# In-projection of a hybrid encoder block: the recurrence's transfers and last products issued by GpSimd, the value norms made beside the memory's keys, two fixed value tiles, the second values last

## The chip, the core and the metric

The kernel runs on 1 core of one Trainium2 chip. Its five engines run side by side, each an instruction stream of its own in a fixed order: TensorE (PE: matrix products; PEld is its weight loading), VectorE (DVE), ScalarE (ACT), GpSimd (POOL) and SyncE (SP). SyncE only issues transfers (DMAs) here; GpSimd computes and issues some. An engine whose next instruction waits, for an operand, a buffer or a transfer, holds everything behind it. The metric is the device time of one execution in microseconds (us). One execution was recorded by the hardware profiler; its rows are quoted below.

## The reference

One layer over 2048 tokens of width 1024, in float32, cut to what the change touches:

```python
xn = rmsnorm(h, norm_mix_g[l])
proj = xn @ w_in[l]
q, k, v, u, y = jnp.split(proj, [512, 1024, 1536, 2048], axis=-1)
q = rope(q, positions)
k = rope(k, positions)
attn = dilated_mixture_attention(q, k, v)
uc = centred_depthwise_conv(u, conv_w[l], conv_b[l])
rec = bidirectional_rglru(uc, ...) * gelu(y)
h = h + concatenate([attn, rec]) @ w_out[l]
```

`bidirectional_rglru` makes two gates of the convolved u in each direction, scans forward and backward over the 2048 tokens and adds the two scans. Cross-attention into 256 memory tokens, an MLP and a last norm follow; neither they nor the attention itself are touched.

## The kernel before

**Products.** Each float32 operand is split in a high part h (rounded by ACT) and a low part l (the rest, by VectorE or GpSimd), and each product is three: h h, l h, h l (`mm3`, L119 to L121). For the weights, SyncE loads 256 KB of w_in into a ring of three buffers `wraw` (L224), ACT makes wh (L225), and wl is made by GpSimd or VectorE in turn (L226).

**Stages of the first 704 us.** The tokens are taken in two blocks of 1024. Block 0's units U and Y come first (a unit is 256 columns of w_in, for 1024 tokens). Then `memory_kv` makes keys and values of the memory, whose last product ends at 141.3 us, and block 1's units U follow. Then come block 1's units Y, v0, k0, q0, v1, k1, q1, with the recurrence `lru` as side work: a generator from which each step of a unit draws 1.3 steps on average. Then x of block 0 is loaded and split again (`x_block`: L315, ACT L320, DVE L321), block 0's units v0 to k1 with the rest of `lru` follow, then the loads of attention head 0 (`load_head`: q and k by GpSimd, L175 and L178), and block 0's last unit q1. Attention's first scores are L750, on `kc`, copies of the keys by GpSimd (L696); L754 on VectorE takes them up.

**Order.** A scheduler sets each engine's order at build time, by the order in which the program is written and priorities; the banks of PSUM (m, b, a) and the buffers of each tile then decide who waits for whom.

**Value norms.** The v units need the sum of squares of each column of the scaled value weights. Before, unit v0 and unit v1 of block 1 each made them when their own weights came: ACT squares (L140, tile vsq), GpSimd adds (L142, vss), four one-column products with a ones vector (L149), a copy, rstd on GpSimd (L115, L116), and a row form through a diagonal dg (L160) and a product (L163, L164). A value tile v (L451) is divided into high and low halves in `vb` (one buffer: memset L454 by GpSimd, L456, L457) and stored by L460.

**Recurrence.** For each of 4 channel tiles (ct) and 4 chunks of 512 tokens, `conv` loads u (L485), makes uc (first tap GpSimd L489, three more VectorE L491) and splits it; `gates` makes products in bank a and ACT's tanh (tr L513, ti L516). Conv runs two chunks ahead of the gates. After each second chunk `forward` scans (L531), and at a channel tile's end `backward` scans back (L536), GpSimd adds the two (L539), gy is loaded (L543), VectorE multiplies (L544) and rec is stored (L545). All these transfers, and the gate weights gr (L469), are SyncE's; gy has two buffers, so a load waits until the rec stored from its buffer has landed.

**Rope.** q and k units are turned by VectorE (L376 to L381), split (rh by ACT L385, rl by VectorE L386) and stored by SyncE (L387, L388).

Of the kernel before, what the change touches and what calls it, by code (L numbers as in the profile page):

```python
# [11 lines left out]
AF = mybir.ActivationFunctionType  # L12
# [12 lines left out]
VW = 130  # L25
# [14 lines left out]
def hybrid_block(ctx: ExitStack, tc: tile.TileContext, prm, x, xT, mem, memT, pos, masks, w_in, gate_w,  # L40
# [61 lines left out]
    nhalf = small("nhalf", [P, 4])  # L102
    pool.memset(nhalf, -0.5)
    ones = small("ones", [P, 1])
    pool.memset(ones, 1.0)
    all1 = small("all1", [P, P])
    pool.memset(all1, 1.0)
    dsc = small("dsc", [P, 4])
    hpi = small("hpi", [P, 1])
# [96 lines left out]
    with ExitStack() as s12:  # L206
# [10 lines left out]
        def unit_steps(src, r, sums=None):  # L217
            for kk in range(2):
                h = wr.tile([P, 4, 256], F32R, tag="wh", name="wh", bufs=4)
                l = wr.tile([P, 4, 256], F32R, tag="wl", name="wl", bufs=4)  # L220
                r.append((h, l))
                for k in range(0, 4, 2):
                    t = wr.tile([P, 2, 256], F32, tag="wraw", name="wraw", bufs=3)
                    dma(t, src[:, 4 * kk + k:4 * kk + k + 2, :])  # L224
                    act.activation(h[:, k:k + 2, :], t, AF.Copy)  # L225
                    (dve if k else pool).tensor_tensor(l[:, k:k + 2, :], t, f32(h[:, k:k + 2, :]), op=ALU.subtract)  # L226
                    for i in range(2 if sums else 0):
                        c = 4 * kk + k + i
                        sums.add(t[:, i, :], gmix[:, c:c + 1])
                    yield  # L230

        def unit_w(src, lazy=False, sums=None):

            r = []
            steps = unit_steps(src, r, sums)
            get = lambda k, c: (r[k // 4][0][:, k % 4, c], r[k // 4][1][:, k % 4, c])
            if lazy:
                return get, steps
            for _ in steps:
                pass  # L240
            return get

# [189 lines left out]
        def v_unit(W, X, B, n2, step, sums):  # L432

            for th in range(2):
                for m2 in range(2):
                    o = ps("mmb")
                    v = p2.tile([P, 512], F32, tag="r0", name="v")
                    for z in range(2):
# [6 lines left out]
                        if sums:  # L445
                            sc = slice(2 * n2, 2 * n2 + 2)
                            sums.columns(svc[:, sc])
                            sums.rows(svr[n2], "a")
                            dve.reciprocal(dsc[:, sc], svc[:, sc])
                            sums = None  # L450
                        dve.scalar_tensor_tensor(v[:, 256 * z:256 * z + 256], oz, rsb[:, r:r + 1], svr[n2],  # L451
                                                 op0=ALU.mult, op1=ALU.mult)
                    vb = p2.tile([P, 8, VW], F16, tag="vb", name="vb", bufs=1)
# [1112 lines left out]
```

## Time and profile before

| what | value |
|---|---|
| median of 3 runs | 2867.53 us (2866.56 to 2873.28) |
| the profiled execution | 2870.64 us |
| its span, first to last instruction | 2868.9 us |
| mean granted TensorE clock | 0.952 |
| TensorE busy, 0 to 100 us | 88.5 us |
| memory's last product ends | 141.3 us |
| the projection's last product ends | 662.6 us |
| first scores begin | 691.0 us |

In the prediction's rows, a wait is read "engine, line, <- what came last: us in total, times, longest". A row of a group has the line, engine, operation, tiles written <- read, shape and count, then busy us and mean ns, then the idle time just before it and what ended it. In the windows, each engine has its busy us and, in brackets, its instructions; PEclk is the clock granted to TensorE as a share of full speed, DMA the busy share of the 16 DMA engines. A row of the timeline starts with the start time and the duration, in us. SPq is SyncE's queue.

### The profile page before, as it was taken

To read this page: it belongs to the slowest core of one execution; us is meant where nothing else is said; L and a number is where in the kernel's file an instruction comes from. 1 tells how busy PE (TensorE), PEld (TensorE's weight loads), DVE (VectorE), ACT (ScalarE), POOL (GpSimd) and SP (SyncE) were. 2 spreads that over 40 slices of the span, in tenths; PEclk is the share of its full clock that TensorE was granted. 3 is DMA by queue.
4 is the path that set the end of the run, shared out by engine and by line. 5 is a ranking of instruction groups with operands and counts; after the bars stand their busy time and mean duration, and the time that the engine had idled before them with its cause. 6 is when DMAs were issued, how large, how long until landed. Compare 5 with 4: busy or idle time off the path is not lost. (4 is left out here: it accounts for less than half of the span.)

```text
span 2868.9 us, 40008 instructions
## 1 busy us (share of the span) xinstructions
PE 2585.6 (90%) x14104; PEld 2186.2 (76%) x14104; DVE 2027.9 (71%) x3376; ACT 1285.1 (45%) x2366; POOL 1256.8 (44%) x884
## 2 busy tenths in 40 slices
PE   8899785884889998999997999899998999999997
PEld 6778675774889998787875788778886777777876
DVE  7547676764778878546578544665548999999997
ACT  6438545452556666335433333433333333333342
POOL 2222121211544442451145555646656766666662
PEclk9999897987889999899998999999999999999999
DMA  6433344336677784653243333343335222212213
GB/s 214 144 125 98 116 113 141 101 106 186 180 184 210 201 206 124 202 170 102 97 159 121 108 113 107 113 144 109 109 114 205 71 84 81 81 67 89 77 49 118
DMA packets 258045, 368.43 MB, mean 128 GB/s; under 512 B 85683, under 2 KB 132019, under 8 KB 254773
## 3 DMA queue, kind: packets, MB, share of 16 engines
q1 hardware_dynamic: 253556, 338.62, 37.4%
q0 software_dynamic: 4288, 27.27, 3.8%
q8 instruction: 111, 1.82, 0.3%
q14 instruction: 90, 0.73, 0.1%
HBM read 251.19 MB, written 114.63 MB: 128 GB/s over the span
## 5 line engine op out<-in xcount | busy, mean ns | idle before, releaser
L1299 ACT ACTIVATE c<-raw 128x512 fp32r<-128x512 f32 x162 | 101.8, 632 | 274.0 <-PE m L120 137.4
L1149 ACT ACTIVATE wh<-wr 128x512 fp32r<-128x512 f32 x128 | 80.9, 632 | 288.9 <-PE m L120 145.9
L1150 POOL TENSOR_TENSOR wl<-wr,wh 128x512 fp32r<-128x512 f32 x96 | 144.7, 1508 | 146.3 <-ACT wh L1149 146.3
L757 ACT ACTIVATE sm<-sm,obp 128x256 f32<-128x256 f32 (+1 forms) x384 | 161.4, 467 | 46.2 <-DVE obp L754 40.0
L1150 DVE TENSOR_TENSOR wl<-ws,wh 128x512 fp32r<-128x512 f32 x96 | 82.2, 856 | 126.5 <-ACT wh L1149 117.6
L754 DVE CUSTOM_DVE_ANT_0 sm<-a,msk 128x256 f32<-128x256 f32 (+1 forms) x384 | 131.0, 371 | 31.3 <-PE a L751 27.5
L226 POOL TENSOR_TENSOR wl<-wraw,wh 128x512 fp32r<-128x512 f32 x48 | 70.3, 1467 | 166.5 <-ACT wh L225 157.6
L1171 DVE TENSOR_TENSOR c<-m,c 128x512 f32<-128x512 f32 x64 | 44.2, 690 | 139.9 <-PE m L121 137.9
L769 ACT ACTIVATE ph<-b 128x512 f16<-128x512 f32 (+1 forms) x192 | 100.4, 523 | 95.2 <-PE b L766 90.3
L119 PE MATMUL m<-xh,wh 128*128 128x512 f32 x328 | 131.3, 400 | 7.4 <-ACT xh L320 7.4
L770 DVE SCALAR_TENSOR_TENSOR pl<-b,ph 128x512 f16<-128x512 f32 (+1 forms) x192 | 114.6, 598 | 28.4 <-ACT ph L769 24.5
L120 PE MATMUL m<-xl,wh 128*128 128x512 f32 x328 | 130.1, 397 | 0.7 <-DVE xl L321 0.7
L121 PE MATMUL m<-xh,wl 128*128 128x512 f32 x328 | 130.5, 398 | 0.0
L1300 POOL TENSOR_TENSOR wh<-raw,c 128x512 fp32r<-128x512 f32 x58 | 94.7, 1648 | 76.6 <-ACT c L1299 71.6
L696 POOL TENSOR_SCALAR kc<-kh 128x1024 fp32r<-128x1024 f32 x32 | 68.5, 2141 | 127.7 <-PE a L750 115.6
L766 PE MATMUL b<-prt,sm 128*128 128x128 f32 x640 | 107.8, 283 | 17.3 <-DVE pl L770 9.3
L750 PE MATMUL a<-kc,qb 128*128 128x256 f32 x256 | 108.5, 425 | 5.9 <-DVE obp L754 5.9
L1172 DVE SCALAR_TENSOR_TENSOR c<-c 128x512 f32<-128x512 f32 x96 | 112.4, 1171 | 1.0
L1149 ACT ACTIVATE wh<-ws 128x512 fp32r<-128x512 f32 x96 | 60.3, 628 | 109.0 <-PE m L120 108.0
L121 PE MATMUL m<-t3h,wl 128*128 128x512 f32 x276 | 107.7, 390 | 1.1 <-POOL wl L1150 1.1
L1300 POOL TENSOR_TENSOR wl<-raw,c 128x512 fp32r<-128x512 f32 x58 | 93.3, 1625 | 19.8 <-ACT c L1299 19.8
L751 PE MATMUL a<-kc,qb 128*128 128x256 f32 x256 | 101.6, 397 | 0.0
(571 smaller groups left out, 9731.0 us busy)
## 6 DMA issues: line engine op xcount, KB each, us to landing
wr<-in_w_m SPq DMA_DIRECT2D x64, 512.0 KB
hid_d<-c SPq DMA_DIRECT2D x128, 256.0 KB
wraw<-in_w_in SPq DMA_DIRECT2D x80, 256.0 KB
raw<-in_w_m SPq DMA_DIRECT2D x33, 512.0 KB
rawt<-hid_d SPq DMA_DIRECT2D x26, 512.0 KB
t0h<-hid_d SPq DMA_DIRECT2D x26, 512.0 KB
o_d<-obp SPq DMA_DIRECT2D x16, 528.0 KB
obr<-o_d SPq DMA_DIRECT2D x16, 528.0 KB
```

The costliest lines, as they stand in the source:

```text
L119: pe.matmul(o, ah, bh, start=start, stop=False, **kw)
L120: pe.matmul(o, ah, bl, start=False, stop=False, **kw)
L121: pe.matmul(o, al, bh, start=False, stop=stop, **kw)
L750: pe.matmul(so, q0, kh[:, w0:w0 + 256], start=True, stop=False)
L754: dve.tensor_tensor_reduce(out=sm, in0=sps[:, 256 * z + o0:256 * z + o0 + kw], in1=msk[:, m:m + kw], op0=ALU.add, op1=ALU.min, scale=1.0, ...
L757: exps.append(act.activation(sm, sm, AF.Exp, scale=-1.0, bias=self.obp[:, oc, 65:66]))
L766: pe.transpose(pt[:, c0:c0 + 128], self.sm[:, z, 128 * g:128 * g + 128], idt)
L770: dve.scalar_tensor_tensor(self.pl[:, :w], pt[:, :w], 1024.0, self.ph[:, :w], op0=ALU.mult, op1=ALU.subtract)
L1149: act.activation(h, self.a[n], AF.Copy)
L1150: last[n % 2] = (pool if n % 2 else dve).tensor_tensor(l, self.a[n], f32(h), op=ALU.subtract).ins
L1172: dve.scalar_tensor_tensor(z, z if n < 6 else o, 0.0, z, op0=ALU.max, op1=ALU.mult)
L1300: self.eng[n].tensor_tensor(l[-1], tk, f32(h[-1]), op=ALU.subtract)
```

## The change

- **Transfers.** The recurrence's transfers (gr, u, gy, rec; 52 in all) are issued by GpSimd (`dma_r`) instead of SyncE (`dma`), and the 16 products of gy by GpSimd instead of VectorE.
- **Value norms.** A new function `value_norms` is called twice after `memory_kv`, before block 1's U. It loads the two value weights once more (8 loads of 256 KB in the same ring), squares them in place (16 on ACT), and sums by 32 products of one column, with the squares as TensorE's weights. The v units no longer make norms.
- **Splits.** From the recurrence's stage on (`alone`), all wl splits go to VectorE; 28 leave GpSimd.
- **Value tiles.** `vb` becomes two fixed tiles, their ones set once.
- **Order of the units.** v0, k0, q0, k1, q1, v1 in place of v0, k0, q0, v1, k1, q1, so v1 is the unit behind head 0's loads; `last["store"]`, after which head 0's far value loads may issue, is now a store of block 0's q1, which comes before v1.
- **Small.** `ones` becomes a column of `all1`, small constants share a tile, and the banks of attention are named in another order.

The diff, with one line of context:

```diff
@@ -99,14 +99,13 @@
     cb, gb, lm, ifq = (col(n) for n in ("conv_b", "gate_b", "lam", "invf"))
-    nhalf = small("nhalf", [P, 4])
+    misc = small("misc", [P, 8])
+    nhalf, hpi = misc[:, 0:4], misc[:, 4:5]
     pool.memset(nhalf, -0.5)
-    ones = small("ones", [P, 1])
-    pool.memset(ones, 1.0)
     all1 = small("all1", [P, P])
     pool.memset(all1, 1.0)
+    ones = all1[:, 0:1]
     dsc = small("dsc", [P, 4])
-    hpi = small("hpi", [P, 1])
     pool.memset(hpi, TWO_PI / 4)
@@ -214,31 +213,49 @@
 
-        def unit_steps(src, r, sums=None):
-            for kk in range(2):
-                h = wr.tile([P, 4, 256], F32R, tag="wh", name="wh", bufs=4)
-                l = wr.tile([P, 4, 256], F32R, tag="wl", name="wl", bufs=4)
-                r.append((h, l))
-                for k in range(0, 4, 2):
-                    t = wr.tile([P, 2, 256], F32, tag="wraw", name="wraw", bufs=3)
-                    dma(t, src[:, 4 * kk + k:4 * kk + k + 2, :])
-                    act.activation(h[:, k:k + 2, :], t, AF.Copy)
-                    (dve if k else pool).tensor_tensor(l[:, k:k + 2, :], t, f32(h[:, k:k + 2, :]), op=ALU.subtract)
-                    for i in range(2 if sums else 0):
-                        c = 4 * kk + k + i
-                        sums.add(t[:, i, :], gmix[:, c:c + 1])
-                    yield
-
-        def unit_w(src, lazy=False, sums=None):
+        def unit_w(src, lazy=False):
 
             r = []
-            steps = unit_steps(src, r, sums)
+
+            def steps():
+                for kk in range(2):
+                    h = wr.tile([P, 4, 256], F32R, tag="wh", name="wh", bufs=4)
+                    l = wr.tile([P, 4, 256], F32R, tag="wl", name="wl", bufs=4)
+                    r.append((h, l))
+                    for k in range(0, 4, 2):
+                        t = wr.tile([P, 2, 256], F32, tag="wraw", name="wraw", bufs=3)
+                        dma(t, src[:, 4 * kk + k:4 * kk + k + 2, :])
+                        act.activation(h[:, k:k + 2, :], t, AF.Copy)
+                        (dve if k or alone[0] else pool).tensor_tensor(l[:, k:k + 2, :], t, f32(h[:, k:k + 2, :]),
+                                                                       op=ALU.subtract)
+                        yield
+
             get = lambda k, c: (r[k // 4][0][:, k % 4, c], r[k // 4][1][:, k % 4, c])
             if lazy:
-                return get, steps
-            for _ in steps:
+                return get, steps()
+            for _ in steps():
                 pass
             return get
+
+        def value_norms(p1, n2):
+
+            sm = RowSum(p1, 1, 256)
+            o = [ps("a") for _ in range(2)]
+            for k in range(0, 8, 2):
+                t = wr.tile([P, 2, 256], F32, tag="wraw", name="wraw", bufs=3)
+                dma(t, w_in[4 + n2][:, k:k + 2, :])
+                for i in range(2):
+                    act.activation(t[:, i, :], t[:, i, :], AF.Square, scale=gmix[:, k + i:k + i + 1])
+                for j in range(2):
+                    for i in range(2):
+                        pe.matmul(o[j][:, 0:1], t[:, i, 128 * j:128 * j + 128], ones, start=k + i == 0, stop=k + i == 7)
+            sc = slice(2 * n2, 2 * n2 + 2)
+            sm.r = svc[:, sc]
+            for j in range(2):
+                dve.tensor_copy(svc[:, 2 * n2 + j:2 * n2 + j + 1], o[j][:, 0:1])
+            rstd_of(sm.r, sm.r, 2)
+            sm.rows(svr[n2], "a")
+            dve.reciprocal(dsc[:, sc], svc[:, sc])
 
@@ -429,7 +446,7 @@
 
-        def v_unit(W, X, B, n2, step, sums):
+        def v_unit(W, X, B, n2, step):
 
@@ -442,16 +459,9 @@
                             mm3(oz, X[0][th][k][:, tk], X[1][th][k][:, tk], wh, wl, k == 0, k == 7)
-                        if sums:
-                            sc = slice(2 * n2, 2 * n2 + 2)
-                            sums.columns(svc[:, sc])
-                            sums.rows(svr[n2], "a")
-                            dve.reciprocal(dsc[:, sc], svc[:, sc])
-                            sums = None
                         dve.scalar_tensor_tensor(v[:, 256 * z:256 * z + 256], oz, rsb[:, r:r + 1], svr[n2],
                                                  op0=ALU.mult, op1=ALU.mult)
-                    vb = p2.tile([P, 8, VW], F16, tag="vb", name="vb", bufs=1)
-                    pool.memset(vb[:, :, 64:66], 1.0)
+                    vb = vbs[m2]
                     v3 = v.rearrange("p (h d) -> p h d", h=8)
@@ -466,7 +476,7 @@
                 gr = lr.tile([P, 4, P], F32, tag="u", name="gr", bufs=2)
-                dma(gr, gate_w[:, 4 * ct:4 * ct + 4, :])
+                dma_r(gr, gate_w[:, 4 * ct:4 * ct + 4, :])
                 gh = lr.tile([P, 4, P], F32R, tag="gh", name="gh")
@@ -482,7 +492,7 @@
                 t0 = 512 * zc - 2
-                dma(u[:, lo:hi], u_d[ct, :, t0 + lo:t0 + hi])
+                dma_r(u[:, lo:hi], u_d[ct, :, t0 + lo:t0 + hi])
                 uc = lr.tile([P, 512], F32, tag="uc", name="uc", bufs=3)
@@ -540,9 +550,9 @@
                     gy = lr.tile([P, 512], F32, tag="gy", name="gy", bufs=2)
-                    dma(gy, gy_d[ct, :, 1024 * c + 512 * z:1024 * c + 512 * z + 512])
-                    dve.tensor_tensor(gy, hf[:, sl], gy, op=ALU.mult)
-                    dma(rec_d[ct, :, 1024 * c + 512 * z:1024 * c + 512 * z + 512], gy)
+                    dma_r(gy, gy_d[ct, :, 1024 * c + 512 * z:1024 * c + 512 * z + 512])
+                    pool.tensor_tensor(gy, hf[:, sl], gy, op=ALU.mult)
+                    dma_r(rec_d[ct, :, 1024 * c + 512 * z:1024 * c + 512 * z + 512], gy)
 
@@ -570,7 +580,7 @@
         U, Y = [(0, "u", 0), (1, "u", 1)], [(2, "y", 0), (3, "y", 1)]
-        QKV = [(4, "v", 0), (6, "k", 0), (8, "q", 0), (5, "v", 1), (7, "k", 1), (9, "q", 1)]
+        QKV = [(4, "v", 0), (6, "k", 0), (8, "q", 0), (7, "k", 1), (9, "q", 1), (5, "v", 1)]
 
@@ -583,27 +593,25 @@
                 mark[0] = tc.cur_priority
-                vs = None
-                if kind == "v" and B == 1:
-                    vs = RowSum(p2, 1, 256, rings={
-                        "ss": lambda: p2.tile([P, 512], F32, tag="rl", name="vss", bufs=2),
-                        "dg": lambda: p2.tile([P, 512], F32, tag="rl", name="vdg", bufs=2),
-                        "sq": lambda: p2.tile([P, 512], F32, tag="rh", name="vsq", bufs=2)})
-                W = first if n == 0 and first else unit_w(w_in[wi], sums=vs)
+                W = first if n == 0 and first else unit_w(w_in[wi])
                 step = pace
...
                 elif kind == "v":
-                    v_unit(W, X, B, n2, step, vs)
+                    v_unit(W, X, B, n2, step)
                 else:
...
 
+        vbs = [p2.tile([P, 8, VW], F16, name=f"vb{i}") for i in range(2)]
+        for vb in vbs:
+            pool.memset(vb[:, :, 64:66], 1.0)
         none = iter(())
...
         due = [0.0]
+        alone = [False]
         with sb("xr") as xr_pool:
@@ -614,10 +622,13 @@
                 softplus()
+                for n2 in range(2):
+                    value_norms(p1, n2)
                 t1 = tables(1)
...
             side = lru(lr)
+            alone[0] = True
             block(1, X, t1, Y + QKV, side)
@@ -636,7 +647,7 @@
         mk = s3.enter_context(sb("mk"))
-        psum_phase("psum2", m0=2, r=1, a=3, b=2)
+        psum_phase("psum2", b=2, m0=2, a=3, r=1)
         pw = s3.enter_context(sb("pw"))
```

SyncE's queue from memory's last weight load on, before (w_cv is the memory's weights, vm_d the memory's values stored, w_in at L224 the weights of U):

```order
59 L224 DMA wraw<-in_w_cv 128x512
60 L224 DMA wraw<-in_w_in 128x512 x2
61 L302 DMA vm_d<-eh 256x1x128
62 L302 DMA vm_d<-el 256x1x128
63 L224 DMA wraw<-in_w_in 128x512 x2
64 L302 DMA vm_d<-eh 256x1x128
65 L224 DMA wraw<-in_w_in 128x512
66 L302 DMA vm_d<-el 256x1x128
67 L224 DMA wraw<-in_w_in 128x512
68 L302 DMA vm_d<-eh 256x1x128
```

The same place after the change (L246 is the load in `value_norms`; the weight load is now L227):

```order
60 L246 DMA wraw<-in_w_in 128x512 x2
61 L319 DMA vm_d<-eh 256x1x128
62 L319 DMA vm_d<-el 256x1x128
63 L246 DMA wraw<-in_w_in 128x512
64 L319 DMA vm_d<-eh 256x1x128
65 L319 DMA vm_d<-el 256x1x128
66 L319 DMA vm_d<-eh 256x1x128
67 L319 DMA vm_d<-el 256x1x128
68 L246 DMA wraw<-in_w_in 128x512 x2
69 L319 DMA vm_d<-eh 256x1x128
70 L319 DMA vm_d<-el 256x1x128
71 L246 DMA wraw<-in_w_in 128x512 x3
```

Eight loads for the norms now stand ahead of U's weight loads, which follow the last row, in the same ring of three buffers.

GpSimd's queue before, at the end of the second channel tile (L539 adds the two scans, L489 is a conv's first tap):

```order
66 L539 TENSOR_TENSOR ti<-ti 128x1024 x2
67 L454 MEMSET vb 128x8x2
68 L481 MEMSET u 128x2
69 L226 TENSOR_TENSOR wl<-wraw,wh 128x512 x2
70 L454 MEMSET vb 128x8x2
71 L489 TENSOR_SCALAR uc<-u,prt 128x512 x2
72 L226 TENSOR_TENSOR wl<-wraw,wh 128x512 x2
73 L489 TENSOR_SCALAR uc<-u,prt 128x512
```

The same place after the change, from behind the first add on (L549 is the second add, L553 and L555 the transfers of gy and rec, L554 the product, L499 the conv's first tap, L495 its u load):

```order
79 L554 TENSOR_TENSOR gy<-ti,gy 128x512 x2
80 L555 DMA rec_d<-gy 128x512 x2
81 L549 TENSOR_TENSOR ti<-ti 128x1024
82 L491 MEMSET u 128x2
83 L495 DMA u<-u_d 128x513
84 L553 DMA gy<-gy_d 128x512 x2
85 L554 TENSOR_TENSOR gy<-ti,gy 128x512
86 L555 DMA rec_d<-gy 128x512
87 L554 TENSOR_TENSOR gy<-ti,gy 128x512
88 L555 DMA rec_d<-gy 128x512
89 L553 DMA gy<-gy_d 128x512 x2
90 L499 TENSOR_SCALAR uc<-u,prt 128x512
```

Between the adds and the next conv's first tap there now stand the products, the stores and the next loads of gy, which GpSimd takes one by one.

GpSimd's queue before, at the loads of head 0 (q to qb, k to kh and kl, then the key copies kc):

```order
91 L226 TENSOR_TENSOR wl<-wraw,wh 128x512 x2
92 L539 TENSOR_TENSOR ti<-ti 128x1024 x2
93 L175 DMA qb<-q_d_64 128x2048
94 L178 DMA kh<-k_d_66 64x2048 x2
95 L178 DMA kl<-k_d_66 64x2048 x2
96 L696 TENSOR_SCALAR kc<-kh 128x1024
97 L696 TENSOR_SCALAR kc<-kl 128x1024
```

The same place after the change:

```order
113 L549 TENSOR_TENSOR ti<-ti 128x1024
114 L553 DMA gy<-gy_d 128x512 x2
115 L554 TENSOR_TENSOR gy<-ti,gy 128x512
116 L555 DMA rec_d<-gy 128x512
117 L554 TENSOR_TENSOR gy<-ti,gy 128x512
118 L555 DMA rec_d<-gy 128x512
119 L174 DMA qb<-q_d_64 128x2048
120 L177 DMA kh<-k_d_66 64x2048 x2
121 L177 DMA kl<-k_d_66 64x2048 x2
122 L707 TENSOR_SCALAR kc<-kh 128x1024
```

Head 0's loads now stand behind the last chain of gy and rec.

## The prediction

> **What bounds the kernel now.** I read the busy times on the page first.
>
> ```profile
> span 2868.9 us, 40008 instructions
> PE 2585.6 (90%) x14104; PEld 2186.2 (76%) x14104; DVE 2027.9 (71%) x3376; ACT 1285.1 (45%) x2366; POOL 1256.8 (44%) x884
> ```
>
> TensorE is the bound, idle for a tenth of the span. The busy times by window say where.
>
> ```profile
> core 0: us, PE busy (x) PEld busy (x) DVE busy (x) ACT busy (x) POOL busy (x), PEclk, DMA share, GB/s
> 200.00:300.00 100.00, 97.59 (x518) 83.49 (x517) 64.90 (x80) 70.95 (x100) 25.66 (x29) 1.00 0.36 100
> 300.00:400.00 100.00, 74.98 (x390) 64.13 (x389) 67.50 (x88) 53.39 (x81) 20.17 (x25) 0.88 0.32 97
> 400.00:500.00 100.00, 67.23 (x329) 55.90 (x328) 65.83 (x95) 54.66 (x81) 10.04 (x9) 0.81 0.47 149
> 500.00:600.00 100.00, 76.47 (x355) 63.41 (x354) 72.17 (x98) 53.66 (x73) 16.36 (x14) 0.86 0.35 103
> 660.00:710.00 50.00, 11.92 (x61) 10.41 (x60) 17.27 (x42) 10.76 (x19) 4.60 (x6) 0.62 0.63 180
> ```
>
> While the recurrence runs beside the projection (300 to 600 us) TensorE is busy 67 to 76%, and the granted clock falls to 0.81; from 660 to 710 it hardly works. TensorE's waits from 300 to 710 us (line, releaser: total, times, longest) name the causes:
>
> ```profile
> PE a L119 <- ACT tr L513: 36.8, 4, 11.8
> PE a L750 <- DVE t L378: 28.4, 1, 28.4
> PE m L119 <- ACT wh L225: 20.8, 2, 13.1
> PE a L119 <- ACT ti L516: 11.4, 6, 5.0
> PE m L119 <- DVE v L451: 10.1, 5, 4.9
> PE a L750 <- DVE obp L754: 9.7, 1, 9.7
> ```
>
> About 79 us go inside the projection, 38 us where attention starts. Behind them stands SyncE, which issues in order (280 to 660 us):
>
> ```profile
> SPq L460 <- DVE vb L457: 44.6, 13, 8.4
> SPq L543 <- DMA rec_d<-gy: 32.1, 11, 8.0
> SPq L224 <- POOL wl L226: 30.8, 11, 7.4
> SPq L545 <- DVE gy L544: 27.3, 9, 7.0
> SPq L224 <- DVE wl L226: 18.7, 10, 8.6
> ```
>
> For 59 us it stands at the recurrence's L543 and L545, and weight and x loads queue behind. Every order from attention's first instruction on is unchanged, so only the first 704 us can move. I sum against the profiled execution, 2870.6 us, 1.7 above its span and 3.1 above the median (2867.5); 0.3%, about 8.6 us, is what a measurement can tell from no change.
>
> **Value norms before block 1 (term A).** What goes is the 13.1 us wait for wh: SyncE issued the second value unit's loads late, behind squares and sums. What comes are 8 loads of 256 KB, 16 squares, 32 one-column products and their short tails. TensorE reads the raw tiles itself, so it now decides when a ring buffer comes free. The nearest rows: TensorE's only wait from 137 to 176 us, the ones-product, the square, and one weight load (issued by SyncE, used by ACT).
>
> ```profile
> PE a L163 <- DVE dg L160: 3.8, 2, 2.9
> L149 PE MATMUL a<-ones,ss x20: 166/250/250, 109.7 to 167.2; 128*128 128x1 f32 x20
> L140 ACT ACTIVATE vsq<-wraw,prt x7: 492/495/508, 350.9 to 357.1; 128x256 f32<-128x256 f32 x7
> 140.97 0.33 SPq L224 DMA_DIRECT2D wraw<-in_w_in  x1
> 144.50 0.63 ACT L225 ACTIVATE wh<-wraw 128x512 fp32r<-128x512 f32 x1 [2.30 <-DMA wraw<-in_w_in]
> ```
>
> Load to use takes 3.5 us. Of the 8 norm loads, 3 are resident when memory's last product is done; the others and the first U load go round the three buffers twice more. One round: load 3.5, two squares 1.0, four products 1.0 = 5.5. So U waits 2 x 5.5 + 3.5 + 0.6 = 15.1 us. Bounds: 10 (one round hidden by memory's tail) to 18 (three products' worth of weight loading and semaphores more). Before, U followed memory without a wait for weights, as the first row shows, so nothing hides this: TensorE is busy 97.6% just behind. The clock loss after a gap (0.88 in the window with the 13.1 us, 1.00 in the one before) I take as alike for the gap that goes and the one that comes. A = +15 - 13 - 1 (small waits of the old norms) = +1, from -5 to +5.
>
> **SyncE freed, block 1 (term B).** 52 transfers leave SyncE's queue. Of the ti wait, 5.0 us lie before 400 us with SyncE's queue behind it, and the value tile now has two buffers, so L460 and GpSimd's memset no longer hold their queues. I take -6, from -14 to +6.
>
> **The passage to block 0 (term C).** Two of the four tr waits lie between 430 and 480 us:
>
> ```profile
> PE a L119 <- ACT tr L513: 23.0, 2, 11.8
> ACT xh L320 <- DMA xr<-in_xT: 19.9, 5, 14.8
> 430.09 0.52 SPq L469 DMA_DIRECT2D gr<-in_gate_w  x1
> 439.34 2.25 SPq L315 DMA_DIRECT2D xr<-in_xT  x3
> ```
>
> ACT stands 14.8 us at one x load, with the gates' tanh behind it, because SyncE issued nothing between 430.6 and 439.3 us. With the 7.7 us of wh that is left (20.8 - 13.1), 30.7 us of idle. After the change nothing of the recurrence stands ahead of x in SyncE's queue. What is late next is GpSimd: between a channel tile's last scan and the next conv product stands the chain of adds, loads, products and stores. Its rows, GpSimd then VectorE:
>
> ```profile
> L226 POOL TENSOR_TENSOR wl<-wraw,wh 128x512 fp32r<-128x512 f32 x17 | 27.2, 1607 | 46.4 <-ACT wh L225 42.1 <-DMA v_d<-vb 4.2
> L539 POOL TENSOR_TENSOR ti<-ti 128x1024 f32<-128x1024 f32 x6 | 15.5, 2590 | 11.2 <-DVE ti L536 11.2
> L178 POOL DMA_DIRECT2D kh<-k_d x2 | 1.1, 542 | 0.0
> L536 DVE TENSOR_TENSOR_SCAN ti<-av,ti 128x1024 f32<-128x1024 f32 x6 | 22.1, 3678 | 0.0
> L544 DVE TENSOR_TENSOR gy<-ti,gy 128x512 f32<-128x512 f32 x14 | 16.6, 1206 | 16.0 <-DMA gy<-gy_d 13.3 <-POOL wl L226 2.7
> L531 DVE TENSOR_TENSOR_SCAN ti<-av,ti 128x1024 f32<-128x1024 f32 x6 | 13.9, 2312 | 0.0
> L226 DVE TENSOR_TENSOR wl<-wraw,wh 128x512 fp32r<-128x512 f32 x18 | 13.3, 736 | 13.7 <-ACT wh L225 13.7
> ```
>
> In sum per channel tile: two adds 5.2, four products 6.4 (by L226's 1.607), eight issues at 0.54 4.3, two landings of rec at 2.9 each (32.1 / 11) 5.8, one gy load 3.5: 25 us. Two conv chunks are made ahead, and I estimate, from this count alone, that half of the 25 us falls under them, so 12 us reach VectorE, whose queue has the conv's other taps, with rope and weight splits behind them, and so TensorE. C = 12 - 30.7 - 1 (clock) = -20, from -30 to +5.
>
> **Block 0's units (term D).** The 17 weight splits in this window leave GpSimd for VectorE: 17 x 0.736 = +12.5 us there; the 14 products that leave save 16.6, and the wide L536 scans, 3.68 beside GpSimd against L531's 2.31, may lose less. VectorE has little to gain or lose; the waits left here (79 less 13.1, 30.7 and 5, some 30 us) are mostly its. Reordering k1, q1, v1 costs the same products. D = -5, from -15 to +12.
>
> **Start of attention (term E).** VectorE's stores and GpSimd's queue around 635 to 691 us:
>
> ```profile
> DVE rl L386 <- DMA k_d<-rl: 23.9, 3, 15.3
> 635.36 0.78 POOL L175 DMA_DIRECT2D qb<-q_d  x1
> 637.18 1.05 POOL L178 DMA_DIRECT2D kl<-k_d  x2
> 650.28 2.00 POOL L696 TENSOR_SCALAR kc<-kh 128x1024 fp32r<-128x1024 f32 x1 [12.04 <-PE m L120]
> 690.29 0.68 DVE L378 TENSOR_TENSOR t<-m,sinT 128x512 f32<-128x512 f32 x1
> ```
>
> The first scores need the bank that L378 frees at 691 us, and L378 stands behind rope's rl, which waits 23.9 us for k stores. With v1 as the last unit no rope, and no such store, stands there. What is late next is head 0's q and k: their loads now queue behind GpSimd's last chain, some 20 us later (25 less what overlaps the scan), at 655 instead of 635.4; 13 us to land as before (637.2 to 650.3), two kc copies 4.4: 673 against 691, -18; of the 9.7 us obp wait, behind the same rl's, I take 2. E = -20, from -30 (the wait gone) to +5 (loads slower beside v1's narrow stores and the far value loads, which block 0's last q store now releases before v1).
> The keyword order of the banks and the ones column move nothing: the banks are numbered as before.
>
> Sum: 2870.6 + 1 - 6 - 20 - 5 - 20 = 2820.6, so 2821.
>
> **The rivals.**
> *Nearly all stalls go.* If GpSimd's chain hides wholly, tr, ti, v (36.8 + 11.4 + 10.1 = 58) and the end's 27 go: 2870.6 + 1 - 58 - 27 = 2787. For it: GpSimd is busy only 10 to 25%. Against: VectorE is over 65% busy, with waits of its own.
> *VectorE is the bound.* All splits now stand in its queue behind rope and scans. SyncE's wait for a VectorE split was 1.9 on average, 8.6 at longest; about 4.6 us in each of the seven last units is +32: 2821 + 32 = 2853. For it: 72% busy from 500 us on. Against: the balance of D.
> The Trainium skill (Trainium Architecture — The Big Picture, What this means for kernel authors) says that VectorE and GpSimd contend for a shared port pair by an exclusive lock. L536's 3.68 us beside GpSimd, against 2.31 for L531, agrees; by that rule the 16 products of 1.6 us on GpSimd would hold VectorE for up to 26 us, and the sum would be 2847.
> *The move between queues is worth nothing.* Transfers share the same 16 DMA engines; if what SyncE stood at was slow transfers, not its own order, B and C fall away and the last loads come late (E about 0, and D with it): 2870.6 + 1 = 2872. For it: L543 waits for rec to land, wherever it is issued. Against: 8.7 us with nothing issued at 430 us.
> The Trainium skill (Trainium Kernel Development and Optimization, Key Constraints) has this rule: the queues share the same DMA engines, and issuing from several engines only saves the sequencer's issue time. By it this rival's 2872 would hold; the stretch behind 430 us, which is no issue time, speaks against it.
> *Slower: GpSimd's chain becomes the gate.* It waits in order for rec to land (2.9 on average, 8.0 at longest, at SyncE's L543) and for gy (3.5 in the chain above; 13.3, all of L544's waits for it, if they fell at one load). At those lengths a chain is 2 x 5.1 + 9.8 = 20 us longer; with the slack under the convs used up, four channel tiles pay 80: 2821 + 80 = 2901. It decides from 12.5 us per tile (50 / 4). For it: contention at 660 us, where DMA is busy 63%. Against: means of 2.9 us.
>
> **How the numbers follow.** Forecast 0.58 (2795 to 2845), stalls gone 0.12, VectorE 0.12, queues nothing 0.06, slower 0.12. The range leaves out the slower case, the no-change case and little else: 2782 to 2862. Faster 0.82, same 0.06, slower 0.12.
>
> **What would show it.** Right: a TensorE gap near 142 to 157 us and none of 13 us near 357; SyncE without waits at recurrence lines; ACT's x wait under 5 us; first scores within 15 us of the projection's last product; tr waits near channel-tile ends that go back to GpSimd's conv product. Wrong: tr waits of over 18 us behind GpSimd's gy and rec, wh waits behind VectorE's splits, or scores that wait over 25 us for kc.

## The result and the profile after

The changed kernel is slower: a median of 2891.4 us (2878.4 to 2892.3, 5 runs) against 2866.9 (2866.2 to 2873.3, 5 runs), a ratio of 1.0069 with a 95% interval from 1.0045 to 1.0094. The profiled execution took 2892.3 us, its span is 2890.5. The forecast was 2821.

Two traces with the same orders from attention's first instruction on can be cut there. Before, TensorE starts its 40th product of scores (counted from 0) at 715.0 us; after, at 713.9. So the stage that the change is about ended 1.1 us earlier, where 50 were forecast, and the rest, which the forecast held fixed, went from 2153.9 to 2176.6 us. The loss lies in the rest alone; of the 71.7 us by which the profiled execution missed the forecast, 48.9 are the gain of the first stage that did not come, and 22.7 the rest. First the groups of score products on the key copies kc, of before and of after (the last times are the first and the last start):

```profile
L750 PE MATMUL a<-kc,qb x256: 334/400/601, 711.2 to 1123.3; 128*128 128x256 f32 x128
```

```profile
L761 PE MATMUL a<-kc,qb x256: 379/398/563, 710.1 to 1124.6; 128*128 128x256 f32 x128
```

The two stay together through attention. Compared product by product, the distance is still -1 us at 1500 us, grows steadily from the MLP's start on, and reaches 19 at the last products. That is the MLP. One window of it, before and after (busy us and number of instructions by engine, then the granted clock):

```profile
1600.00:1800.00 200.00, 199.90 (x880) 164.54 (x880) 99.66 (x117) 64.44 (x113) 109.95 (x74) 1.00 0.31 110
```

```profile
1600.00:1800.00 200.00, 200.00 (x859) 161.15 (x858) 91.63 (x113) 64.30 (x111) 106.78 (x71) 1.00 0.32 108
```

TensorE never waits in either, the clock is full in both, yet 859 products fit where 880 did. By their starts, a product of 512 columns follows the last every 226.7 ns before and every 233.3 after (231.6 on average behind 2200 us). In the first 1500 us the projections have 227 to 228 in both kernels. Nothing in the MLP's code is touched.

Inside the first 704 us the waits were exchanged, not removed. TensorE's from 300 to 660 us, and the two behind:

```profile
PE a L118 <- ACT tr L523: 41.0, 6, 17.6
PE m L120 <- DVE wl L229: 15.3, 1, 15.3
PE a L118 <- ACT ti L526: 10.2, 3, 7.0
PE m L118 <- DVE v L462: 9.2, 2, 8.4
PE b L118 <- DVE v L462: 4.2, 1, 4.2
```

```profile
PE b L118 <- DVE v L462: 21.0, 1, 21.0
PE a L761 <- DVE obp L765: 4.8, 1, 4.8
```

Within the projection 79.9 us are waited, against 81.6 before (the prediction's 79 leaves two small waits out). The 13.1 us for wh near 357 are gone, and 17.6 us near 316 have come (ACT's tanh stands behind a weight that lands late), with 15.3 near 604 for a split on VectorE. At attention's start the 28.4 us behind rope became 21.0 us behind the value tiles, and the first scores begin at 696.1 us instead of 691.0.

SyncE's waits from 280 to 660 us show what the move to GpSimd took away and what came:

```profile
SPq L404 <- ACT rh L402: 97.3, 18, 14.2
SPq L227 <- DVE wl L229: 72.7, 26, 12.9
SPq L470 <- DVE vb L467: 53.1, 10, 12.6
```

The 59 us at the recurrence's lines are gone. SyncE now stands 72.7 us for weight buffers that VectorE frees (18.7 by VectorE and 30.8 by GpSimd before), and longer for rope's rh: it was early at lines that were not ready.

### The profile page after: what moved, and what is told of

It reads as the page before. It is cut to its first block, busy times and chain, and to the rows that moved or that the text cites. A ratio compares the mean times of both kernels' runs of the same rounds, so it can differ in the third digit from the quotient of the medians.

```text
span 2890.5 us, 40057 instructions
## 1 busy us (share of the span) xinstructions
PE 2621.3 (91%) x14160; PEld 2200.8 (76%) x14160; DVE 2022.6 (70%) x3390; ACT 1285.8 (44%) x2366; POOL 1261.3 (44%) x895
## 5 line engine op out<-in xcount | busy, mean ns | idle before, releaser
L120 PE MATMUL m<-xh,wl 128*128 128x512 f32 x344 | 137.3, 400 | 15.3 <-DVE wl L229 15.3
L119 PE MATMUL m<-xl,wh 128*128 128x512 f32 x344 | 136.2, 396 | 0.0
L777 PEld LDWEIGHTS b<-prt,sm 128*128 128x128 f32 x640 | 76.2, 145 | 24.3 <-issue 9.2
```

What stands on the lines that cost most here:

```text
L119: pe.matmul(o, ah, bl, start=False, stop=False, **kw)
L120: pe.matmul(o, al, bh, start=False, stop=stop, **kw)
L777: pe.transpose(pt[:, c0:c0 + 128], self.sm[:, z, 128 * g:128 * g + 128], idt)
```

## The experiments

The 40th score product is the marker of the first stage, "rest" the span behind it. (Where an expectation speaks of the start of steady attention, that is some 11 us ahead of the marker: 702.9 us in the changed kernel.) Each time is compared with the kernel before on the chip it ran on; medians of that kernel went from 2867 to 2878 us between chips.

| kernel | 40th score, us | rest, us | ratio of times to before (95%) |
|---|---|---|---|
| before | 715.0 | 2153.9 | 1 |
| changed | 713.9 | 2176.6 | 1.0069 (1.0045 to 1.0094) |
| e1_repeat | 713.3 | 2174.2 | 1.0046 (1.0029 to 1.0063) |
| e2_consts | 717.7 | 2174.5 | 1.0047 (1.0031 to 1.0062) |
| e3_sync | 714.5 | 2173.5 | 1.0052 (1.0032 to 1.0073) |
| e4_v1_mid | 727.6 | 2177.5 | 1.0097 (1.0076 to 1.0119) |
| e5_pad64 | 712.2 | 2153.1 | 0.9973 (0.9952 to 0.9994) |
| e6_packed | 717.1 | 2170.6 | 1.0059 (1.0034 to 1.0084) |
| e7_pad32 | 714.1 | 2178.1 | one run, 2894.0 us |
| e8_split_pool | 720.1 | 2150.6 | 1.0003 (0.9983 to 1.0024) |
| e9_norms_back | 706.0 | 2166.0 | 0.9976 (0.9951 to 1.0001) |
| e10_vb4 | 700.1 | 2154.0 | 0.9935 (0.9912 to 0.9959) |
| e11_order_tiles | 716.5 | 2153.0 | 0.9998 (0.9973 to 1.0023) |
| e12_queue_only | 725.8 | 2150.7 | 1.0020 (0.9997 to 1.0043) |
| e13_vb4_sync | 705.2 | 2154.3 | 0.9931 (0.9908 to 0.9955) |
| e14_vb4_norms_back | 685.6 | 2158.7 | 0.9943 (0.9920 to 0.9965) |
| e15_no_rec0 | 691.5 | 2143.0 | one run, 2836.2 us |

The marker differs by up to 4 us between executions that should agree (713.9, 713.3, and 717.7 of e2_consts), and memory's last product, ahead of nearly all that the edits touch, ends between 138.6 and 143.1 us; differences below 5 us say nothing.

### Is the slow MLP the program's, and which part's?

**e1_repeat**: the changed kernel, no edit.

> The changed kernel once more. In its trace the first 704 us are no longer than before (steady attention begins at 702.9 against 704.0 us), and the 21.6 us of span are lost behind 1511 us, where 512-column matmuls begin every 233.3 ns instead of 226.7 with the same granted clock. Theory 1, the slow cadence belongs to this program: it returns in this run, at the same place, and the median lies at 2888 to 2893 us. Theory 2, it is a state of single executions that any kernel can fall into: the cadence or the place where it begins differs, and some of the times lie near 2868.

It came back at the same place: 233.3 ns from 1600 us on. It is the program's.

**e2_consts**:

```diff
-    nhalf, hpi = misc[:, 0:4], misc[:, 4:5]
+    nhalf, hpi, ones = misc[:, 0:4], misc[:, 4:5], misc[:, 5:6]
+    pool.memset(ones, 1.0)
...
-    ones = all1[:, 0:1]
...
-        psum_phase("psum2", b=2, m0=2, a=3, r=1)
+        psum_phase("psum2", m0=2, r=1, a=3, b=2)
```

> The changed kernel with the ones vector in its own memory (a column of the constants' tile) instead of the first column of the all-ones tile, and the banks of attention named in the old order. Theory 1a, the slow matmuls come from the ones column or the banks' names: the MLP goes back to 226.7 ns, about 2868 us. Theory 1b, they come from something else in the program, and theory 2, from the execution: 233 ns and 2888 to 2893 us, or as in the repeat.

233.3 ns and a rest of 2174.5: neither the ones column nor the banks' names. e3_sync and e4_v1_mid, below, kept 233.3 ns too. What all of them share is that the constants take 64 bytes per partition less: three small tiles (32 bytes each as placed) became one. Everything laid from the left end of SBUF moved by 64 bytes, and what is laid from the right end did not. In the built programs the MLP's activations t begin at byte 18080 before and 18016 after, and its weights wh at 208800 in both. By 128, t stood at 32 beside weights at 32, and now stands at 96.

**e5_pad64**:

```diff
+    pad = s7.enter_context(sb("pad"))
+    pad.tile([P, 16], F32, name="pad")
     jp = s7.enter_context(sb("jp"))
```

> The changed kernel with 64 bytes per partition left empty ahead of the MLP's activations (tiles t and c), so that they lie where they lay before the change. Every kernel with the packed constants so far had 233.3 ns in the MLP. Theory 1c: packing the constants moved the left half of SBUF by 64 bytes and the right half (the MLP's weights wh and wl) not, and TensorE takes 6.7 ns longer where one operand lies 64 bytes off the other by 128. Then 226.7 ns come back, the part behind the start of attention takes 2154 us as before, and the time is within 0.4% of the kernel before. Rival 1d, the norms, splits or value tiles leave a state that slows the matmuls behind: 233.3 ns stay, and the time is 0.5 to 0.7% above the kernel before.

**e6_packed**: the kernel before with the constants' lines of the change alone.

> The kernel before with only the constants packed (misc tile, ones as a column of the all-ones tile). Theory 1c: 233.3 ns in the MLP and 18 to 23 us more than the kernel before, with the first 704 us unchanged. Rival 1d: no change.

The same window of e5_pad64, then of e6_packed:

```profile
1600.00:1800.00 200.00, 200.00 (x884) 165.64 (x883) 100.11 (x118) 65.58 (x115) 114.09 (x75) 1.00 0.33 111
```

```profile
1600.00:1800.00 200.00, 200.00 (x858) 161.13 (x858) 95.07 (x114) 64.34 (x112) 105.75 (x72) 1.00 0.32 108
```

884 products with the empty bytes, 858 in the kernel before with nothing but its constants packed. The padding takes the rest from 2176.6 to 2153.1 us and the ratio from 1.0046 (e1_repeat; 1.0069 at first) to 0.9973; the packing alone adds 16.7 us of rest, a little less than the 18 expected, and makes the kernel before 0.59% slower. So the shift by 64 bytes is the cause, shown in both directions, and the rival 1d is out.

**e7_pad32**: as e5_pad64 with 32 bytes (`pad.tile([P, 8], ...)`).

> The changed kernel with 32 empty bytes instead of 64 ahead of the MLP's activations. Theory 1c in its strict form (any offset between the operands by 128 costs): 233.3 ns. In its mild form (only the middle of 128 bytes, 64 off, costs): 226.7 ns. Rival 1d: 233.3 ns.

With t at byte 0 by 128 and the weights at 32 it is 233.3 ns again. So, of products of t and wh or wl, those with both operands at 32 by 128 take 226.7 ns, and those with t at 96 or at 0 and the weights at 32 take 233.3. In block 1's U products of the changed kernel both operands stand at 96, and 227 ns are seen. That fits the strict form, any offset between the two, for these positions.

From 2250 to 2800 us the traces do not bear that form out product by product. There t meets in turn the weights and other tiles of the MLP, c, which move with t. In the changed kernel a product of t and c (both at 96) takes 229.8 ns on average to the next start (gaps up to 300 ns) and one of t and weights (96 and 32) 233.8; in e7_pad32 it is the other way round, 234.9 with both at 0 and 230.9 with t at 0 and the weights at 32; before, all take 227. So the shift costs, but which positions of the two cost how much, and why, is not shown.

### What the parts are worth in the first stage

**e3_sync**: all five lines of the recurrence back to `dma` and `dve`, in the changed kernel.

> The changed kernel with the recurrence's transfers issued by SyncE again and the gy products made by VectorE again; the rest as changed. If the queue move is worth what the prediction said (terms B and C), attention starts 20 to 30 us later than in the changed kernel, so at 723 to 733 us. Rival: what SyncE stood at were transfers, and the move gives nothing: 700 to 708 us. For the cadence, theory 1b: 226.7 ns if the transfers by GpSimd are what slows the matmuls behind, else 233.

714.5 against 713.9 and 713.3: no difference at the marker, the rival. But the trace shows a balance and not nothing. At the product that TensorE begins at 640.0 us in the changed kernel, e3_sync is 10.5 us ahead. Then TensorE stands 31.1 us (21.0 in the changed kernel) until VectorE has taken up a value product. VectorE waits there for a load of gy that SyncE issues at 660.9 us, when a rec store has landed, beside which GpSimd had issued head 0's loads from 641.1 us on. (In the changed kernel GpSimd issues rec, gy and then head 0's loads, and that gy load waits 1.95 us for rec.) VectorE's wait, 630 to 700 us, and SyncE's, 636 to 670:

```profile
DVE gy L554 <- DMA gy<-gy_d: 24.2, 2, 23.6
```

```profile
SPq L553 <- DMA rec_d<-gy: 20.7, 2, 19.6
```

So with v1 last the move costs some 10 us within the projection and gives them back at its end. **e12_queue_only** is the other direction, those five lines alone in the kernel before.

> The kernel before with the move to GpSimd alone (the recurrence's transfers and the gy products). Undoing the move inside the changed kernel shifted the 40th score by 0 to 1 us. Theory (the rule of the skill, the prediction's rival on queues): worth nothing, the 40th score at 711 to 719 us and the time within 0.3% of before. Rival (the prediction's terms B and C): 685 to 700 us. The slower rival: over 730 us.

725.8 against 715.0, outside the theory's and the gain's range and short of the slower rival's 730, at a ratio whose interval just reaches 1. GpSimd's queue and TensorE's wait of e12_queue_only:

```profile
648.96 0.55 POOL L175 DMA_DIRECT2D qb<-q_d  x1
...
668.08 1.98 POOL L696 TENSOR_SCALAR kc<-kh 128x1024 fp32r<-128x1024 f32 x1 [16.50 <-DMA kh<-k_d]
```

```profile
PE a L750 <- DVE t L378: 36.7, 1, 36.7
```

Head 0's loads stand behind the last gy and rec chain, 13.6 us later than the 635.36 of before, and the wait before the scores is 36.7 instead of 28.4.

**e4_v1_mid**:

```diff
-        QKV = [(4, "v", 0), (6, "k", 0), (8, "q", 0), (7, "k", 1), (9, "q", 1), (5, "v", 1)]
+        QKV = [(4, "v", 0), (6, "k", 0), (8, "q", 0), (5, "v", 1), (7, "k", 1), (9, "q", 1)]
```

> The changed kernel with the units in the old order (v1 before k1 and q1, q1 last). In the changed kernel TensorE waits 21.0 us for the v1 tile's store just before attention, where before it waited 28.4 us for rope. Theory: the end is worth the same in both orders, so attention starts within 4 us of the changed kernel's 703 us. Rival (the prediction's term E): the old order costs 20 us more, 723 us.

13.7 us dearer, so between the two theories. **e11_order_tiles** puts the order and the two value tiles alone into the kernel before (with the constants packed and the 64 empty bytes).

> The kernel before with the new order of the units (v1 last) and the two fixed value tiles alone (constants packed to make room, 64 empty bytes ahead of the MLP's activations). Going back to the old order inside the changed kernel cost 13.7 us at the 40th score. Theory: the order of units and the value tiles are worth that by themselves: the 40th score at 698 to 705 instead of 715.0. Rival: the gain needs the other parts: 710 to 718.

716.5: no gain, the rival. TensorE waits for v there, 24.0 us at longest, and VectorE ahead of it 23.3 us for a load of gy, as in e3_sync. So the new order and the move need each other: the move alone costs 10.8 us at the marker (e12_queue_only), the order alone exchanges rope's wait for gy's, and together they come out even.

**e10_vb4**, on e5_pad64, asks about the changed kernel's wait of 21.0 us behind the value tiles:

```diff
-                    vb = vbs[m2]
+                    vb = vbs[(m2 + 2 * th) % len(vbs)]
...
+        vx = s12.enter_context(sb("vx"))
+        vbs += [vx.tile([P, 8, VW], F16, name=f"vb{i}") for i in (2, 3)]
+        for vb in vbs[2:]:
+            pool.memset(vb[:, :, 64:66], 1.0)
         block(0, X, tabs, QKV[-1:], none)
```

> The changed kernel with the 64 empty bytes, and with four value tiles instead of two in the last unit v1, so that none of its four tiles waits for a store. Theory: ACT's 25 us wait for the value store to land is what holds TensorE for 20.0 us ahead of the last values, and behind it head 0's keys are next, landing about 8 us earlier than the scores begin now: first score at 680 to 688 instead of 692.3, the 40th at 702 to 708 instead of 712.2. Rival: the stores and loads share the transfers' time, and the first score stays within 4 us of 692.

ACT in the changed kernel, 640 to 705 us, and TensorE's waits of e10_vb4, 640 to 740:

```profile
ACT vb L466 <- DMA v_d<-vb: 25.2, 1, 25.2
```

```profile
PE b L118 <- DVE v L462: 7.6, 2, 6.6
PE a L766 <- DMA kl<-k_d: 4.1, 1, 4.1
PE b L781 <- DVE pl L785: 2.6, 2, 2.3
PE a L765 <- DMA kh<-k_d: 2.2, 1, 2.2
```

The wait for the store goes, head 0's keys come last, as theory said: first score at 683.4, the 40th at 700.1, 12.1 us earlier and 2 below the range. This kernel beats both: 0.9935.

The store that ACT waits for in the changed kernel was late in its queue. Its tile was ready at 658.6 us, but SyncE stood until 680.1 at two of head 0's value loads, of 65 KB each, which stand ahead of v1's stores now that v1 is the last unit:

```profile
658.50 8.32 SPq L184 DMA_DIRECT2D v<-v_d  x1
666.86 13.19 SPq L185 DMA_DIRECT2D v<-v_d  x1
680.14 4.55 SPq L470 DMA_DIRECT2D v_d<-vb  x2
```

In the kernel before the issues of the same two took 6.50 and 3.34 us. Whether stores ahead of these loads would do as well as four tiles was not tried.

**e8_split_pool**, on e5_pad64:

```diff
-                        (dve if k or alone[0] else pool).tensor_tensor(...)
+                        (dve if k else pool).tensor_tensor(...)
```

> The changed kernel with the 64 empty bytes and half of the recurrence stage's weight splits back on GpSimd. If the splits on VectorE are what took back the gain of the first 704 us (the rival on VectorE, priced at 32 us; in the changed kernel SyncE's ring of raw weights waits 82.7 us for them), steady attention starts 15 to 30 us earlier than with the padding alone, whose start is expected at 703 to 708 us. If not, within 5 us of it.

The opposite: 7.9 us later (2.9 of them were there when memory ended, 141.5 against 138.6 us), and 0.3% slower than with the splits on VectorE (1.0003 against 0.9973; the intervals overlap a little). TensorE's 15.1 us wait for a split, which e5_pad64 has too, is gone there, and those for tr sum to 31.2 us instead of 42.0, but those for ti and v grew by 24. Its waits from 300 to 730 us:

```profile
PE a L118 <- ACT tr L523: 31.2, 8, 7.9
PE b L118 <- DVE v L462: 28.3, 2, 16.0
PE a L118 <- ACT ti L526: 25.3, 6, 8.1
PE m L118 <- DVE v L462: 13.0, 3, 9.1
```

**e9_norms_back**, on e5_pad64: `value_norms` and its call removed, the RowSum of the v units as before.

> The changed kernel with the 64 empty bytes (its TensorE reaches the 40th score product at 712.2 us, the kernel before at 715.0), and with the value norms made in block 1's v units again, as before the change. Theory: the norms beside the memory are dearer than what they save, since U now starts 16.8 us later in a stage where TensorE is 97 to 99% busy, and the 13.1 us wait that they were to remove came back as other waits for weights: the 40th score comes 8 to 17 us earlier, at 695 to 704. Rival (the prediction's term A): a wash, within 5 us of 712.

706.0, 6.2 us earlier, just outside the rival and short of the theory. In the profiled execution attention then lost those again, and the times say 0.9976 against 0.9973: no difference. **e14_vb4_norms_back** does the same on e10_vb4.

> The changed kernel with the 64 empty bytes, four value tiles in the last unit, and the value norms made in the v units as before. Norms back gave 6 us at the 40th score and none in the time. Theory: about 6 us again at the 40th score, 691 to 698, and the time 0 to 6 us below the one with four tiles. Rival: the kept wait for weights eats it, 698 to 704.

685.6, 14.5 us earlier at the marker and ahead of the theory's range; 0.9943 against 0.9935 in time. That the norms beside the memory cost the stage something is seen twice; that undoing them makes the kernel faster is not seen.

**e13_vb4_sync**: e3_sync's edit on e10_vb4.

> The changed kernel with the 64 empty bytes and four value tiles in the last unit (its 40th score stands at 700.1 us and its time 0.65% below the kernel before), and with the recurrence's transfers on SyncE and its gy products on VectorE as before the change. Alone, the move to GpSimd cost 11 us at the 40th score, since head 0's loads stand behind GpSimd's chain. Theory: with the value stores no longer in the way that cost shows again, and undoing the move brings the 40th score to 690 to 697 us. Rival: the loads are late for want of transfer time, 698 to 704.

705.2, later by 5: the theory falls, and the rival's range is missed too, on its far side. As in e3_sync, TensorE stands 31.0 us for a value product and VectorE 23.6 us for gy, which four value tiles do not touch. The times are equal (0.9931 and 0.9935).

**e15_no_rec0**, on e10_vb4, leaves out the first channel tile's load of gy, the multiplication by it, and the store at that place (rec of that tile is stored earlier, by the y units):

```diff
-                    dma_r(gy, gy_d[ct, ...])
-                    pool.tensor_tensor(gy, hf[:, sl], gy, op=ALU.mult)
-                    dma_r(rec_d[ct, ...], gy)
+                    if ct:
+                        dma_r(gy, gy_d[ct, ...])
+                    pool.tensor_tensor(gy, hf[:, sl], gy if ct else hf[:, sl], op=ALU.mult)
+                    if ct:
+                        dma_r(rec_d[ct, ...], gy)
```

> As the one with four value tiles, but for the first channel tile no gy is loaded, the product takes the scans' sum twice, and rec is not stored there; rec of that tile is filled earlier, from block 1's and block 0's first y rows, so what is left out is the first channel tile's output. In the changed kernel TensorE waits 17.6 us near 316 us, where three weight loads take 9 to 14 us to land, just behind four rec stores, gy loads and four k stores. Theory: the transfers' burst is what makes the loads late, and without these eight transfers the wait falls below 9 us. Rival: the ring of raw weights is freed late by VectorE's splits, and the wait stays at 14 to 20 us.

The wait of 18.1 us in e10_vb4 became 13.2, between the two. In this one run some 5 us belong to the traffic of gy and rec; the other 13 stay without it. The three loads issued at 313.7 to 317.2 us behind four key stores still gave ACT nothing before 325.4. Whether those stores or the ring holds them stays open.

## Why the prediction was wrong, point by point

**The step that failed first**, and the one that made the kernel slower, is the sentence "The keyword order of the banks and the ones column move nothing", with the sum's premise that only the first 704 us can move. The front lists the packed constants as a small item, and I costed the edit by its instructions, at nothing. Its cost is where it puts everything else: 17 us alone (e6_packed), 23 in the changed kernel, and the whole of the measured loss. The order of instructions, on which I rested that premise, does not show addresses. The larger part of the miss, 48.9 of 71.7 us, is the gain that terms B, C and E promised in the first stage.

**Terms B and C, -26, measured as a balance of 0 to -1 within the changed kernel (e3_sync) and at +11 alone (e12_queue_only).** I read SyncE's 59 us at rec and gy as the cause of TensorE's waits. The proof I gave did come: ACT's wait for x, from 400 to 480 us, fell from 19.9 us to

```profile
ACT xh L337 <- DMA xr<-in_xT: 2.0, 2, 1.2
```

and TensorE's gaps between 428 and 480 us sum to 16 instead of 31. But the weight loads, no longer held behind the recurrence, came up against their ring, against key stores and VectorE, and the same time was waited near 316 and 604 us. The balance is what the rival "the move between queues is worth nothing" forecast, but not for its reason: two differences of some 10 us cancel in it. The Trainium skill (Trainium Kernel Development and Optimization, Key Constraints) has the rule that issuing from several engines only saves the sequencer's issue time. The marker, 0 to 1 us apart in e3_sync, agrees with it, but the two differences below it are more than issue time: the queue that issues also sets what is issued first, and VectorE's 23.6 us for gy came of that.

The chain on GpSimd was a gate once, for 8.4 us, where term C had put 12. A conv's first tap stood behind gy loads that waited for rec, VectorE for the tap, and TensorE at 448.9 us for a value tile behind it:

```profile
445.09 0.54 POOL L553 DMA_DIRECT2D gy<-gy_d  x1 [3.01 <-DMA rec_d<-gy]
445.67 0.77 POOL L499 TENSOR_SCALAR uc<-u,prt 128x512 f32<-128x512 f32 x1
```

```profile
446.47 0.75 DVE L501 SCALAR_TENSOR_TENSOR uc<-u,prt,uc 128x512 f32<-128x512 f32 x1 [8.50 <-POOL uc L499]
```

**Term A, +1, measured at +6 at the marker (e9_norms_back), and at +14 with four tiles (e14_vb4_norms_back).** The delay of U was sized well by luck: U begins at 158.4 us, 16.8 after memory's last product begins (15.1 forecast), but not because TensorE waits for the ring. From 141.7 us on it waits 4.1 us and is busy 12.6, of these 11.3 with the 32 one-column products, which have 64 rows in the trace, at a mean granted clock of 0.66. The sum had 8 us for these products.

```profile
L251 PE MATMUL a<-all,wraw 128*128 128x1 f32 x64 | 11.3, 307 | 2.3 <-ACT wraw L248 2.3
```

What failed is the 13 us on the other side, which I counted as saved; they were late weights, and late weights came back at 316 us.

**Term D, -5.** As a whole it was not measured. The splits on VectorE, which it counted as 12.5 us of cost there, are worth 5 to 8 us at the marker (e8_split_pool), at the edge of what the marker tells. The rival that made VectorE the bound, 32 us dearer, did not come. Nor did VectorE's scans slow beside GpSimd's 16 products: the backward scan, 3.68 us on average before (L536, 300 to 660 us), took 3.33 after.

**Term E, -20.** This part was wrong against the kernel before: the first scores begin 5 us later, not 18 earlier. Half of the mechanism came. Head 0's loads were issued at 663.1 us in the changed kernel (655 forecast), and the old order behind them would have cost 13.7 us more (e4_v1_mid). But I wrote "no rope, and no such store, stands there": v1 has stores of its own, two tiles to wait for them with, and head 0's near value loads ahead of them in SyncE's queue, which the term did not price. Against the kernel before, the order alone gains nothing (e11_order_tiles), and four tiles gain the 12 us (e10_vb4).

**The rival on the slower side** named GpSimd's chain, at 2901. That gate was seen once, at 8.4 us, and not at 20 us in each channel tile (from 300 to 660 us VectorE waits 11.0 us in all for first taps); that the time came near 2901 is chance. The kernel is slower for a reason that none of the cases held.

## What to carry to other kernels

When an edit changes the size of anything that is allocated early, compare the addresses of both operands of the busiest products, not only the order of instructions: 64 bytes cost more here than all waits of the stage gave back. A wait of an in-order queue is a cause only if what stands behind it is otherwise ready; ask of each load that it frees which buffer, store and engine it meets next, and undo the part alone to price it. Where undoing it changes nothing, compare the two traces product by product: here two differences of 10 us cancelled. A last unit whose stores go through two buffers exchanges one wait for another: look at what stands ahead of its stores in their queue, and give it as many tiles as it has stores before it is moved in front of a stage.

## What the hardware showed that was not expected

- At full granted clock, 512-column products of t and wh follow each other every 226.7 ns with both operands at byte 32 by 128 of their partition and every 233.3 ns with t at 96 or 0 and the weights at 32, from 1600 to 1800 us; with what follows it made 17 to 24 us of 2154.
- While TensorE waited near 316 us, ACT could use a weight load of 256 KB 14.2 us after SyncE began to issue it (316.84 to 331.00 us; the issue alone took 4.2), where the row of before had 3.5. Without the eight transfers of e15_no_rec0 it was 11.7, and the wait fell from 18.1 to 13.2 us.
- The issue of one load of 65 KB (L185 after) held SyncE's queue for 13.2 us, with the value tiles' stores behind it; the same load took 3.34 before.
- The kernel before itself had medians of 2867 to 2878 us on different chips, as much as many of the differences here, so only comparisons on one chip count.
